# TensorE in the order of the source inside a latent-attention stage, with maxima, turns and keys at other places

## The chip, the cores and the metric

The kernel runs on one core of a Trainium2 chip. A core has five engines, each with its own queue of instructions: TensorE (PE) for matrix products and transposes, VectorE (DVE), ScalarE (ACT), GpSimd (POOL) and SyncE (SP), which here starts most of the transfers (DMA). Engines wait for each other by semaphores. PE writes to PSUM, a small memory of eight banks, here one tile `PB` of eight banks of 512 floats for each of 128 partitions; In this kernel DVE and ACT read PSUM, POOL does not. All else lies in SBUF, here mostly in two large tiles, `arena_r` and `arena_f`. The metric is the time of one execution in microseconds (us), lower is better.

## The reference

A backbone of two layers over 1024 latent tokens and 256 context tokens, width 1024. Layer 0 is windowed attention, layer 1 latent attention; each adds its gated result to the stream. The change touches layer 1 alone:

```python
q = (rms_norm(cq, q_norm) @ w_uq).reshape(b, n, B_HEADS, B_NOPE + B_ROPE)
kv = (rms_norm(ckv, kv_norm) @ w_ukv).reshape(b, n, B_HEADS, B_NOPE + B_V)
...
s = (jnp.einsum("bqhd,bkhd->bhqk", qn, kn)
     + jnp.einsum("bqhd,bkd->bhqk", qr, kr)).astype(F32) * scale
p = jax.nn.softmax(s, axis=-1).astype(v.dtype)
return jnp.einsum("bhqk,bkhd->bqhd", p, v)
```

There are 16 heads; a query and a key have 64 entries of their own and 32 rotated ones, a value has 64. Each of the 1024 latent queries sees all 1280 keys, context first. The result is multiplied by a gate, projected by `w_out`, added to the stream and normalised.

## The kernel before, in words

The first thousand microseconds compute layer 0 and the projections of layer 1. The stage of the change starts near 1000 us and ends near 1540; the output projection of the last tiles follows.

In this stage the work is cut into 32 units (class `UnitB`). Unit `i` is one head and one half of the queries (512): two heads make a pair, so four units in a row belong to one pair of heads, in the order head 0 first half, head 0 second half, head 1 first half, head 1 second half. A unit does, in terms of the code's names:

- `prep`: loads the queries, already split into a high and a low part (two DMAs).
- `top(b)`, four times, for 128 queries each: three matmuls (L1294) into banks 0 to 2 give rough scores against all 1280 keys, and DVE takes their maximum in one reduction over 1280 columns (L1298). All tops share the same three banks, so a top has to wait until the reduction of the one before has read them.
- `shift`: a transpose (L1302) turns the maxima, and four short ACT instructions (L1305) write them as extra rows of the queries, so that the scores come out already lowered by the maximum.
- `score(c)` for the ten chunks of 128 keys: three matmuls (`mm3`, L126, L127, L128: high by high, low by high, high by low) into one of the banks 3, 4, 5 in turn, then the exponential on ACT (L1313), then an addition on POOL (L1317, L1320) that sums the denominators.
- `PV`: ten matmuls (L1328) of the exponentials with the values into bank 6. Each takes half of PE's columns, even chunks the lower and odd chunks the upper half.
- `fin`: a copy on ACT (L1342) and an addition on DVE (L1343) join the two halves.
- `fin2`: four transposes (L1353) of the summed denominators, which need POOL's last addition, a sum on DVE (L1354) and, for the second head of a pair, a reciprocal and two copies on ACT (L1357, L1362).
- `fin3`, for the second head of a pair alone: four transposes (L1371), a product on DVE (L1372), a product with the gate on POOL (L1374) and a store.

The loop over the units lays these out over the ten scores `c` of a unit: tops and shift of the next unit, `fin2` and `fin3` of the one before, and the next pair's keys. `make_K` makes those in the third unit of a pair, in three pieces of 512, 512 and 256 keys (`KEYB`): for each piece two `mm3` write one bank with both heads, 64 partitions each, and for each head a cast on ACT (L121) and a subtraction on DVE (L122) split it. `make_V` makes the values of four heads in every eighth unit, in five pieces. Banks are handed out in turn by the objects `pst4` (3, 4, 5), `psv` (6) and `psx` (7, for the transposes).

Order: the framework records the instructions and its scheduler sets the order on every engine by its own costs and priorities, unless a part of the kernel is put under `tc.manual_schedule`, in which the engines named keep the order of the source. An earlier stage is under it, this one is not. Waits on semaphores are then placed by the framework wherever two instructions use the same place in a tile.

Of the kernel before, what the change touches and what calls it, by code (L numbers as in the profile page):

```python
# [33 lines left out]
class Ring:  # L34
# [6 lines left out]
    def next(self):  # L41
        b = self.bufs[self.i % len(self.bufs)]
        self.i += 1
        return b
# [15 lines left out]
def kernel(ctx: ExitStack, tc: tile.TileContext, t, out, dbg=None):  # L60
    nc = tc.nc
# [57 lines left out]
    def split(hi, lo, src, lo_eng=None):  # L119

        nc.scalar.copy(hi, src)  # L121
        (lo_eng or nc.vector).tensor_sub(lo, src, hi.bitcast(F32))  # L122

    def mm3(o, a, b, first, last):
        (ah, al), (bh, bl) = a, b
        nc.tensor.matmul(o, ah, bh, start=first, stop=False)  # L126
        nc.tensor.matmul(o, al, bh, start=False, stop=False)  # L127
        nc.tensor.matmul(o, ah, bl, start=False, stop=last)  # L128
# [345 lines left out]
    psv = Banks(5)  # L474
# [390 lines left out]
    in_order = tc.manual_schedule()  # L865
# [45 lines left out]
    for ui, u in enumerate(units):  # L911
# [7 lines left out]
        nu = units[ui + 1] if ui + 1 < len(units) else None  # L919
# [299 lines left out]
    pst4 = Banks(3, 4, 5)  # L1219
    psv = Banks(6)  # L1220
# [18 lines left out]
    def make_V(quad):  # L1239
        for tp in range(NP):  # L1240
            ps = pst4()
            for j in range(2):
                ti = 2 * tp + j
                for k in range(2):
                    mm3(
                        ps[:, j * 256 : j * 256 + 256],
                        [ckvT[:, s, k, ti * 128 : ti * 128 + 128] for s in range(2)],
                        [ukV[:, s, k, quad * 256 : quad * 256 + 256] for s in range(2)],
                        k == 0, k == 1,
                    )  # L1250
            nc.scalar.copy(Vq[:, 2 * tp : 2 * tp + 2], shp(ps, 2, 4, 64))
            yield

    def make_K(pair):
        for n0, n in KEYB:
            ps = pst4()
            for k in range(2):
                mm3(
                    ps[:, 0:n],
                    [ukK[:, s, k, pair * 128 : pair * 128 + 128] for s in range(2)],  # L1260
                    [ckvT[:, s, k, n0 : n0 + n] for s in range(2)],
                    k == 0, k == 1,
                )
            for e in range(2):
                kt = kTb[(2 * pair + e) % 3]
                split(kt[0:64, 0, n0 : n0 + n], kt[0:64, 1, n0 : n0 + n], ps[64 * e : 64 * e + 64, 0:n])
            yield
# [119 lines left out]
    def wo_pieces():  # L1387
        ring = Ring(F, [45, 47, 49], 512)
        pieces = [(k, slice(c * 512, c * 512 + 512)) for k in range(8) for c in range(2)]
        staged = []  # L1390
        for i in range(len(pieces) + 2):
            if i < len(pieces):
                k, cs = pieces[i]
                st = ring.next()
                load(out=st, in_=t["b_w_out"][k * 128 : k * 128 + 128, cs])
                staged.append((k, cs, st))
            if i >= 2:
                k, cs, st = staged.pop(0)
                split(WoB[k][:, 0, cs], WoB[k][:, 1, cs], st)
                yield  # L1400
# [102 lines left out]
    for _ in make_K(0):  # L1503
        pass
# [30 lines left out]
    out_fill = out_tiles()  # L1535
    wo_fill = wo_pieces()
    kfill = vfill = iter(())
    for ui, u in enumerate(units):
        pu = units[ui - 1] if ui else None
        nu = units[ui + 1] if ui + 1 < NU else None  # L1540
        nnu = units[ui + 2] if ui + 2 < NU else None
        if ui % 4 == 2 and u.pair < 7:
            kfill = make_K(u.pair + 1)
        if ui and ui % 8 == 0:
            vfill = make_V(u.pair // 2)
        for c in range(NT):
            if nu and ui and c in (1, 4, 6):
                nu.top({1: 1, 4: 2, 6: 3}[c])
            if nu and c == 8:
                nu.shift()  # L1550
            if nnu and c == 3:
                nnu.prep()
            u.score(c)
            if nnu and c == 9:
                nnu.top(0)
            if c == 9:
                u.PV()
                u.fin()
            if pu and c == 3:
                pu.fin2()  # L1560
            if pu and c == 5:
                pu.fin3()
            if ui % 4 == 2 and c in (1, 3, 5):
                next(kfill, None)
            if ui and ui % 8 == 0 and c in (1, 2, 4, 6, 7):
                next(vfill, None)
            if ui % 2 and 3 <= ui < 25 and c == 0 or 25 <= ui < 29 and c in (0, 5):
                next(wo_fill, None)
            if ui == NU - 1 and c in (0, 3, 5, 6, 7, 8, 9):
                next(out_fill, None)  # L1570
    for _ in wo_fill:
        pass
    u = units[-1]
# [81 lines left out]
```

## Time and profile before

| | |
|---|---|
| median of three runs | 1631.81 us (1630.6 to 1632.72) |
| profiled execution, its time | 1630.86 us |
| its span | 1628.6 us |
| PE busy over the span | 1577.6 us (97%) |
| DVE, ACT, POOL busy | 947.7, 803.8, 815.5 us |
| 1100 to 1200 us: PE, DVE, ACT, POOL busy | 99.78, 52.14, 55.56, 68.42 us |

The profile is one execution. Busy time of PE is the time in which a matmul was under way; successive matmuls overlap, so their lengths add up to more than the time from start to start. In the records each matmul of L1328 appears twice, so ten of them are x20. The granted clock is the share of its full clock that PE was given; it is 1.00 for nearly all of the run and lower in a few short stretches.

### The profile page before, as it was taken

The page shows a single profiled execution, that of the slowest core. Times are in us where ns is not written, and L with a number is a line of the kernel's source. Part 1 is how long each engine was busy: PE and PEld are TensorE (multiplying, and loading weights), DVE is VectorE, ACT ScalarE, POOL GpSimd, SP SyncE. Part 2 cuts the span into 40 slices and gives each one's busy share as a digit, 9 for nine tenths or more (in the row PEclk, how much of TensorE's full clock was granted, in tenths as well). Part 3 has the DMA queues.
Part 4 walks back from the last instruction along what each step waited for, and adds up shares of the span by engine and source line. Part 5 has one row for each costly group of instructions (what it writes and reads, how often), then busy time and mean ns, then how long its engine had stood idle before and what let it go on. Part 6 is the DMA issues. An engine that isn't in the chain of part 4 may idle for free.

```text
span 1628.6 us, 23522 instructions
## 1 busy us (share of the span) xinstructions
PE 1577.6 (97%) x8156; PEld 1213.2 (74%) x8156; DVE 947.7 (58%) x1719; ACT 803.8 (49%) x1715; POOL 815.5 (50%) x871
## 2 busy tenths in 40 slices
PE   6899999989999999999999999999999999999998
PEld 2788788777888888878887887566666666666687
DVE  2766778637777777768353016655545455455354
ACT  2511221249777777777233335555555555555421
POOL 2653355235453333335154423686777768668410
PEclk8999999989999999999999999999999999999999
DMA  8435644564343333243138613111110110122151
GB/s 302 159 124 176 205 145 152 175 187 120 95 142 97 92 92 91 78 147 120 45 107 281 188 55 110 55 56 33 40 56 20 55 33 33 56 72 70 47 162 65
DMA packets 122430, 176.72 MB, mean 109 GB/s; under 512 B 11452, under 2 KB 71484, under 8 KB 122312
## 3 DMA queue, kind: packets, MB, share of 16 engines
q1 hardware_dynamic: 115032, 164.31, 31.7%
q10 hardware_dynamic: 7280, 10.92, 2.1%
q8 instruction: 64, 1.05, 0.3%
q14 instruction: 54, 0.44, 0.1%
HBM read 129.04 MB, written 46.15 MB: 108 GB/s over the span
## 4 chain that ended last, share of the span: by engine, by line
PE 82%; ACT 4%; DVE 4%; issue 3%; DMA 3%; POOL 3%; SPq 0%; ACTq 0%; POOLq 0%; DVEq 0%
PE PB L126 18%; PE PB L128 17%; PE PB L127 17%; PE PB L1328 9%; PE PB L570 5%; PE PB L1294 4%; PE PB L560 4%; PE PB L533 2%; PE PB L534 2%; DMA arena_f<-a_w_in 1%; PE PB L1353 1%; DVE arena_f L344 1%; ACT arena_f L581 1%; ACT arena_f L1313 1%; DMA arena_f<-x 1%
## 5 line engine op out<-in xcount | busy, mean ns | idle before, releaser
L126 PE MATMUL PB<-arena_r 128*128 128x512 f32 (+3 forms) x1632 | 608.6, 373 | 3.3 <-ACT arena_r L205 2.1
L127 PE MATMUL PB<-arena_r 128*128 128x512 f32 (+3 forms) x1632 | 596.8, 366 | 2.9 <-POOL arena_r L727 2.2
L128 PE MATMUL PB<-arena_r 128*128 128x512 f32 (+3 forms) x1632 | 595.0, 366 | 0.2 <-DVE arena_r L122 0.2
L126 PEld LDWEIGHTS PB<-arena_r 128*128 128x128 f32 (+1 forms) x1632 | 310.7, 190 | 91.6 <-issue 32.9
L1320 POOL TENSOR_TENSOR arena_f<-arena_f 128x512 f32<-128x512 f32 x252 | 327.1, 1298 | 75.1 <-ACT arena_f L1313 60.0
L128 PEld LDWEIGHTS PB<-arena_r 128*128 128x128 f32 (+1 forms) x1632 | 310.0, 190 | 49.0 <-DVE arena_r L122 0.4
L127 PEld LDWEIGHTS PB<-arena_r 128*128 128x128 f32 (+1 forms) x1632 | 310.9, 191 | 45.1 <-POOL arena_r L727 2.7
L1298 DVE TENSOR_REDUCE arena_f<-PB 128x1 f32<-128x1280 f32 x128 | 190.4, 1487 | 104.2 <-PE PB L1294 101.7
L1313 ACT ACTIVATE arena_f<-PB 128x512 f32<-128x512 f32 x320 | 189.0, 597 | 125.2 <-PE PB L128 112.8
L122 DVE TENSOR_TENSOR arena_r<-PB,arena_r 128x512 fp32r<-128x512 f32 (+4 forms) x245 | 158.7, 655 | 124.2 <-ACT arena_r L121 122.4
L122 POOL TENSOR_TENSOR arena_r<-arena_f,arena_r 128x512 fp32r<-128x512 f32 x80 | 111.3, 1405 | 173.1 <-ACT arena_r L121 169.5
L121 ACT CAST arena_r<-PB 128x512 fp32r<-128x512 f32 (+4 forms) x245 | 135.4, 557 | 68.1 <-PE PB L560 39.3
L540 DVE CUSTOM_DVE_ANT_0 arena_f<-PB,arena_f,small 128x256 f32<-128x256 f32 (+1 forms) x288 | 145.4, 523 | 32.1 <-PE PB L534 25.3
L1328 PE MATMUL PB<-arena_f 128*64 128x512 f32 x640 | 157.1, 600 | 0.0
L541 ACT ACTIVATE arena_f<-arena_f,small 128x640 f32<-128x640 f32 (+2 forms) x160 | 118.9, 744 | 27.8 <-DVE small L540 26.9
L570 PE MATMUL PB<-arena_r 128*128 128x512 f32 x336 | 120.8, 436 | 4.5 <-ACT arena_f L581 4.1
L344 DVE SCALAR_TENSOR_TENSOR arena_f<-arena_f,small 128x512 f32<-128x512 f32 x98 | 116.3, 1231 | 2.6 <-DMA arena_f<-ada_w 2.2
L121 ACT CAST arena_r<-arena_f 128x512 fp32r<-128x512 f32 (+1 forms) x120 | 69.7, 608 | 76.8 <-DMA arena_f<-a_w_in 26.4
L560 PE MATMUL PB<-ident,arena_f 128*128 128x128 f32 x672 | 104.9, 273 | 0.5 <-ACT arena_f L541 0.3
L1328 PEld LDWEIGHTS PB<-arena_f 128*64 128x64 f32 x640 | 43.6, 136 | 80.9 <-issue 79.5
L1294 PE MATMUL PB<-arena_r 96*128 96x512 f32 (+1 forms) x384 | 99.8, 368 | 0.3 <-DVE arena_f L1298 0.2
L560 PEld LDWEIGHTS PB<-ident,arena_f 128*128 128x128 f32 x672 | 82.6, 140 | 15.0 <-ACT arena_f L541 1.5
(163 smaller groups left out, 1723.0 us busy)
## 6 DMA issues: line engine op xcount, KB each, us to landing
arena_r<-q_d SPq DMA_DIRECT2D x148, 128.0 KB, 2.9
arena_f<-ada_w SPq DMA_DIRECT2D x64, 256.0 KB, 3.3
arena_f<-a_w_in SPq DMA_DIRECT2D x40, 256.0 KB, 3.1
arena_f<-ada_w SPq DMA_DIRECT2D x16, 512.0 KB, 7.3
arena_f<-x SPq DMA_DIRECT2D x16, 512.0 KB, 3.5
q_d<-arena_f SPq DMA_DIRECT2D x16, 512.0 KB, 3.5
qn_d<-arena_f SPq DMA_DIRECT2D x16, 512.0 KB, 5.7
arena_r<-qn_d SPq DMA_DIRECT2D x32, 256.0 KB, 3.5
```

The source lines that it names most:

```text
L121: nc.scalar.copy(hi, src)
L122: (lo_eng or nc.vector).tensor_sub(lo, src, hi.bitcast(F32))
L126: nc.tensor.matmul(o, ah, bh, start=first, stop=False)
L127: nc.tensor.matmul(o, al, bh, start=False, stop=False)
L128: nc.tensor.matmul(o, ah, bl, start=False, stop=last)
L560: nc.tensor.transpose(pt[:, h, :], self.Ps[h][:, ci * 128 : ci * 128 + 128], ident)
L570: nc.tensor.matmul(self.pv, V[:, self.chunks[ci], self.g, :], PT[:, s], start=ci == 0 and s == 0, stop=ci == self.m - 1 and s == 1,)
L1294: nc.tensor.matmul(psm[:, n0 : n0 + n], self.qT[0:96, 0, b * 128 : b * 128 + 128], kt[0:96, 0, n0 : n0 + n], start=True, stop=True,)
L1298: nc.vector.reduce_max(self.mx[:, 96 + b : 97 + b], psm[:, 0:TOK], AX.X, negate=True)
L1313: nc.scalar.activation(E, S, AF.Exp)
L1320: eng.tensor_add(self.acc, self.acc, E)
L1328: nc.tensor.matmul(self.pv[p : p + 64], Vq[:, c, self.h % 4, :], self.E.pop(c), start=c < 2, stop=c >= NT - 2)
```

## The change

It has three parts.

First, the loop over the units is put under `tc.manual_schedule` for PE alone: PE now does what the source says, in that order; the scheduler still orders DVE, ACT, POOL and SP, now around a fixed PE. Second, calls move within the loop, and so on PE: the second, third and fourth top (`top(1)`, `top(2)`, `top(3)`) come before scores 1, 3, 5 instead of 1, 4, 6, `shift` before score 9 instead of 8, `fin2` before score 2 instead of after 3, `fin3` before score 6 instead of after 5, the three pieces of keys after scores 2, 4, 7 instead of 1, 3, 5. Third, from the second pair on the keys are written to bank 6 (`psv`), which the product with the values uses, instead of one of the three banks of the scores.

```diff
     def make_K(pair):
         for n0, n in KEYB:
-            ps = pst4()
+            ps = pst4() if pair == 0 else psv()
...
+    in_order = tc.manual_schedule(engines={nc.tensor.engine})
+    in_order.__enter__()
     for ui, u in enumerate(units):
...
         for c in range(NT):
-            if nu and ui and c in (1, 4, 6):
-                nu.top({1: 1, 4: 2, 6: 3}[c])
-            if nu and c == 8:
+            if pu and c == 2:
+                pu.fin2()
+            if pu and c == 6:
+                pu.fin3()
+            if nu and ui and c in (1, 3, 5):
+                nu.top({1: 1, 3: 2, 5: 3}[c])
+            if nu and c == 9:
                 nu.shift()
...
             if c == 9:
                 u.PV()
                 u.fin()
-            if pu and c == 3:
-                pu.fin2()
-            if pu and c == 5:
-                pu.fin3()
-            if ui % 4 == 2 and c in (1, 3, 5):
+            if ui % 4 == 2 and c in (2, 4, 7):
                 next(kfill, None)
...
+    in_order.__exit__(None, None, None)
```

What this does to the order, at three places. On PE, the end of a unit that makes keys and the next unit's first scores; L1328 is the product with the values, 128x512 in L126 to L128 a score. Before:

```order
L1328 MATMUL PB<-arena_f 64x512 x6
L126 MATMUL PB<-arena_r 128x512
L127 MATMUL PB<-arena_r 128x512
L128 MATMUL PB<-arena_r 128x512
L1328 MATMUL PB<-arena_f 64x512
L126 MATMUL PB<-arena_r 128x512
L127 MATMUL PB<-arena_r 128x512
L128 MATMUL PB<-arena_r 128x512
L1328 MATMUL PB<-arena_f 64x512 x2
```

After:

```order
L1302 MATMUL PB<-ident,arena_f 100x128
L126 MATMUL PB<-arena_r 128x512
L127 MATMUL PB<-arena_r 128x512
L128 MATMUL PB<-arena_r 128x512
L1294 MATMUL PB<-arena_r 128x512 x2
L1294 MATMUL PB<-arena_r 128x256
L1328 MATMUL PB<-arena_f 64x512 x10
```

Two scores of the next unit and a single matmul stood inside the product; now the shift's transpose, the last score and the first top of the unit after next stand ahead of it, and its ten matmuls follow each other.

On PE, the second and third top of an ordinary unit (L1294). Before:

```order
L1294 MATMUL PB<-arena_r 128x512 x2
L1294 MATMUL PB<-arena_r 128x256
L126 MATMUL PB<-arena_r 128x512
L127 MATMUL PB<-arena_r 128x512
L128 MATMUL PB<-arena_r 128x512
L126 MATMUL PB<-arena_r 128x512
L127 MATMUL PB<-arena_r 128x512
L128 MATMUL PB<-arena_r 128x512
L126 MATMUL PB<-arena_r 128x512
L127 MATMUL PB<-arena_r 128x512
L1294 MATMUL PB<-arena_r 128x512 x2
L1294 MATMUL PB<-arena_r 128x256
```

After:

```order
L1294 MATMUL PB<-arena_r 128x512 x2
L1294 MATMUL PB<-arena_r 128x256
L126 MATMUL PB<-arena_r 128x512
L127 MATMUL PB<-arena_r 128x512
L128 MATMUL PB<-arena_r 128x512
L126 MATMUL PB<-arena_r 128x512
L127 MATMUL PB<-arena_r 128x512
L128 MATMUL PB<-arena_r 128x512
L1294 MATMUL PB<-arena_r 128x512 x2
L1294 MATMUL PB<-arena_r 128x256
```

Eight matmuls of scores stood between the two tops, now six.

On DVE, a unit that makes keys, from the second top's maximum (L1298) on; L122 with 64x512 or 64x256 is the subtraction that ends the split of one head's piece of keys, L1354 the sum of `fin2`. Before:

```order
L122 TENSOR_TENSOR arena_r<-PB,arena_r 64x512
L1354 TENSOR_REDUCE small<-PB 128x4
L122 TENSOR_TENSOR arena_r<-PB,arena_r 64x512
L1298 TENSOR_REDUCE arena_f<-PB 128x1
L122 TENSOR_TENSOR arena_r<-PB,arena_r 64x512
L1298 TENSOR_REDUCE arena_f<-PB 128x1
L122 TENSOR_TENSOR arena_r<-PB,arena_r 64x512
L122 TENSOR_TENSOR arena_r<-PB,arena_r 64x256
L1298 TENSOR_REDUCE arena_f<-PB 128x1
L122 TENSOR_TENSOR arena_r<-PB,arena_r 64x256
```

After:

```order
L1354 TENSOR_REDUCE small<-PB 128x4
L1298 TENSOR_REDUCE arena_f<-PB 128x1
L122 TENSOR_TENSOR arena_r<-PB,arena_r 64x512 x2
L1298 TENSOR_REDUCE arena_f<-PB 128x1
L122 TENSOR_TENSOR arena_r<-PB,arena_r 64x512 x2
L122 TENSOR_TENSOR arena_r<-PB,arena_r 64x256 x2
L1298 TENSOR_REDUCE arena_f<-PB 128x1
```

The first piece's two subtractions stood ahead of the second top's maximum and now stand behind it; those of the second piece stand behind the third top's maximum, and the last piece's ahead of the first maximum of the unit after next. On ACT the second cast of each piece stands behind the exponential of a score that PE reaches just before the next piece (score 4, score 7) or just before the shift (score 8).

## The prediction

> **What bounds the kernel now.** I read the busy shares first, then the table of windows for four neighbouring units, then the timelines of TensorE (PE), VectorE (DVE) and ScalarE (ACT) inside a unit. A row of windows gives the stretch, its length, the busy time and count of PE, weight loads, DVE, ACT and POOL, the granted clock, DMA share and GB/s; a row of a timeline gives start, length, engine, line, what it does, and the idle time before it with what ended it.
>
> ```profile
> span 1628.6 us, 23522 instructions
> PE 1577.6 (97%) x8156; PEld 1213.2 (74%) x8156; DVE 947.7 (58%) x1719; ACT 803.8 (49%) x1715; POOL 815.5 (50%) x871
> 1199.04:1214.29 15.25, 15.12 (x72) 9.69 (x72) 8.05 (x8) 8.38 (x19) 12.74 (x11) 1.00 0.19 61
> 1214.29:1228.74 14.45, 14.45 (x68) 9.31 (x67) 7.24 (x6) 7.68 (x17) 11.91 (x11) 1.00 0.19 65
> 1228.74:1263.86 35.12, 35.01 (x157) 21.75 (x156) 18.89 (x20) 18.85 (x40) 23.89 (x19) 1.00 0.08 23
> 1199.04:1263.86 64.82, 64.57 (x295) 40.75 (x294) 34.19 (x34) 34.92 (x72) 48.54 (x39) 1.00 0.13 41
> ```
>
> PE is busy 64.57 of 64.82 us in a group of four units at full clock, and DVE about half. So time can be won only where PE's own work gets shorter, and any wait of PE is lost in full. The profiled execution took 1630.86 us, 2.3 beyond its span and 0.95 below the median of the runs, 1631.81.
>
> One ordinary unit on PE, from one product with the values (L1328, ten instructions, two records each) to the next, with DVE's reductions (L1298: a maximum; L1354: the sum in fin2) behind it:
>
> ```profile
> 1214.29 4.51 PE L1328 MATMUL PB<-arena_f 128*64 128x512 f32 x20
> 1218.73 0.50 PE L126 MATMUL PB<-arena_r 100*128 100x512 f32 x1
> ...
> 1219.53 0.73 PE L1294 MATMUL PB<-arena_r 96*128 96x512 f32 x3
> 1220.10 0.40 PE L126 MATMUL PB<-arena_r 100*128 100x512 f32 x1
> ...
> 1222.17 0.60 PE L1353 MATMUL PB<-ident,arena_f 128*128 128x128 f32 x4
> 1222.53 0.84 PE L1294 MATMUL PB<-arena_r 96*128 96x512 f32 x3
> 1223.20 0.39 PE L126 MATMUL PB<-arena_r 100*128 100x512 f32 x1
> 1223.43 0.39 PE L127 MATMUL PB<-arena_r 100*128 100x512 f32 x1
> ...
> 1225.05 0.75 PE L1294 MATMUL PB<-arena_r 96*128 96x512 f32 x3
> ```
> ```profile
> 1219.55 0.68 DVE L1343 TENSOR_TENSOR arena_f<-PB,arena_f 64x512 f32<-64x512 f32 x1 [3.66 <-ACT arena_f L1342]
> 1222.81 0.69 DVE L1354 TENSOR_REDUCE small<-PB 128x4 f32<-128x512 f32 x1 [1.01 <-PE PB L1353]
> 1223.42 1.48 DVE L1298 TENSOR_REDUCE arena_f<-PB 128x1 f32<-128x1280 f32 x1
> 1225.84 1.49 DVE L1298 TENSOR_REDUCE arena_f<-PB 128x1 f32<-128x1280 f32 x1 [0.94 <-PE PB L1294]
> ```
>
> Starts of following rows give PE's prices: 4.44 for ten value products, 0.80 for the first score of a unit, 0.57 for a top, 0.69 for a score (three matmuls of 0.23), 0.36 for fin2's four transposes. The round trip of a top: started at 1225.05, its reduction starts 0.79 later and takes 1.49; the earlier reduction ended at 1224.90 and the next top started 0.15 after that. Start to start, two tops need 0.79 + 1.49 + 0.15 = 2.43 us, which leaves 1.86 between the end of one and the start of the next. Before, 2.67 scores stand there (1223.20 to 1225.05, 1.85 us).
>
> **The value product in one run (a gain).** In the units that make keys the run was cut:
>
> ```profile
> 1243.95 1.07 PE L1328 MATMUL PB<-arena_f 128*64 128x512 f32 x2
> 1244.95 0.32 PE L1302 MATMUL PB<-ident,arena_f 128*100 128x128 f32 x1
> ...
> 1247.21 2.80 PE L1328 MATMUL PB<-arena_f 128*64 128x512 f32 x12
> 1249.94 0.50 PE L126 MATMUL PB<-arena_r 100*128 100x512 f32 x1
> ...
> 1250.83 1.07 PE L1328 MATMUL PB<-arena_f 128*64 128x512 f32 x2
> 1251.83 0.50 PE L126 MATMUL PB<-arena_r 100*128 100x512 f32 x1
> ...
> 1252.73 1.08 PE L1328 MATMUL PB<-arena_f 128*64 128x512 f32 x4
> 1253.74 0.85 PE L1294 MATMUL PB<-arena_r 96*128 96x512 f32 x3
> ```
>
> The pieces cost 1.00 + 2.73 + 1.00 + 1.01 = 5.74 against 4.44: two neighbours share their time, one alone pays for both. That is 1.30 a group. I take the whole possible gain from the group: four units of 14.45, keys of 12 x 0.23 + 6 x 0.12 = 3.5, and fin3's four transposes twice at fin2's 0.36 make 62.0; before takes 64.82. So 2.8 is the most that order can win, fin3's stall included (15.25 - 14.45 - 0.36 = 0.44 each, twice). Units 0 and 1 were cut as 1 + 9, which saves about 1.0 each.
>
> **Maxima at scores 1, 3, 5 (a loss).** Counted from the unit's first score: first top at 0.80, S1, fin2 at 2.06, S2, so the second top could start at 3.11. The first reduction runs 1.59 to 3.08, so the top starts at 3.23. Its reduction runs 4.02 to 5.51 (fin2's sum, 3.08 to 3.77, is out of its way), so the third top starts at 5.66, where two scores would let it start at 3.23 + 0.57 + 1.38 = 5.18. Waits: 0.12 + 0.48 = 0.60, less 0.1 for a switch cost between L1353 and L1294 (0.67 where 0.57 is usual) that goes away: 0.5 in each of the three units of a group that make no keys, 1.5 a group. A unit with values has their matmuls between the tops, so there this is an upper bound.
>
> **Fin2 at score 2, fin3 at 6 (nothing).** Fin2's transposes need POOL's last add, and PE now waits for it in order.
>
> ```profile
> 1215.90 1.27 POOL L1374 TENSOR_TENSOR arena_f<-arena_f,arena_r 128x512 f32<-128x512 f32 x1
> 1217.14 2.62 POOL L1320 TENSOR_TENSOR arena_f<-arena_f 128x512 f32<-128x512 f32 x2
> ```
>
> The last add ends at 1219.76, 1.03 after the score at 1218.73; fin2 comes at 2.06. The cover is 1.0 us. POOL's gating multiply of fin3 and its store to DRAM come two adds earlier: the same work on POOL and SP, and the later adds still end before 2.06. If that cover went, each microsecond late would be PE's. Fin3 stands 3.5 us behind fin2, past its sum, reciprocal and copies. The shift one score later has top 0 and the value product, 5 us, ahead of the next unit's scores.
>
> **Keys in the bank of the product (the large loss).** Three scores shared three banks with the keys; now each piece of keys has one bank, and the next piece (then the value product) must wait until both heads of the last are split.
>
> ```profile
> 1236.85 0.58 ACT L121 CAST arena_r<-PB 64x512 fp32r<-64x512 f32 x1 [0.73 <-PE PB L128]
> 1238.23 0.58 ACT L121 CAST arena_r<-PB 64x512 fp32r<-64x512 f32 x1
> ```
> ```profile
> 1237.46 0.68 DVE L122 TENSOR_TENSOR arena_r<-PB,arena_r 64x512 fp32r<-64x512 f32 x1 [1.21 <-ACT arena_r L121]
> 1239.40 0.69 DVE L122 TENSOR_TENSOR arena_r<-PB,arena_r 64x512 fp32r<-64x512 f32 x1
> ```
>
> Cast, subtraction, cast, subtraction go one after the other: the second cast starts 0.08 after the first subtraction ends (1238.15), so 0.58 + 0.03 + 0.69 + 0.08 + 0.58 + 0.03 + 0.69 = 2.7 us. In the new order DVE takes the second top's reduction first, and ACT takes the second cast of piece 1 behind the exponential of score 7. By the clock of the unit: piece 0 at 3.11 to 4.50, the second top at 4.50, its reduction 5.29 to 6.78, subtraction to 7.47, cast to 8.13, subtraction to 8.85, piece 1 at 9.00. PE would be there at 5.08 + 1.38 = 6.46: a wait of 2.5. Piece 1 ends at 10.39, the third top at 10.97, S5 to S7 at 13.04; the exponential of S7 ends near 13.9, cast 14.5, subtraction 15.22, piece 2 at 15.37: 2.3. Piece 2 ends at 16.09, S8 16.78, S9 and the top 18.2; its second cast, behind the exponential of S8, ends at 18.03 and the subtraction of 0.42 at 18.48, the product starts at 18.63: 0.4. Sum 5.2 a group. Between ends: nothing, if DVE and ACT took the splits at once and two scores hid them, and about 6, if each exponential in ACT's way came late; I take 5.2, since the rows show the chain's length.
>
> **Clock after a wait.** The granted clock drops for 3.41 us after a stretch of 3.41 with much idle time:
>
> ```profile
> 69.67:73.09 3.42, 1.66 (x14) 1.66 (x15) 3.29 (x8) 2.72 (x5) 2.39 (x2) 1.00 0.04 13
> 73.09:76.50 3.41, 3.41 (x31) 3.41 (x30) 3.32 (x8) 1.25 (x2) 0.78 (x2) 1.00 0.00 0
> 342.74:346.15 3.41, 1.52 (x9) 0.97 (x8) 0.00 (x0) 0.23 (x1) 0.00 (x0) 1.00 1.10 250
> 346.15:349.56 3.41, 0.00 (x0) 0.00 (x0) 0.76 (x2) 1.50 (x3) 0.20 (x1) 0.50 1.13 218
> 738.68:742.09 3.41, 1.28 (x10) 1.08 (x10) 3.41 (x7) 2.67 (x6) 1.99 (x4) 1.00 0.32 89
> 742.10:745.51 3.41, 3.18 (x14) 2.83 (x14) 3.17 (x4) 3.06 (x8) 3.24 (x3) 0.50 0.12 38
> ```
> ```profile
> 741.58 0.37 PE L126 MATMUL PB<-arena_r 128*128 128x288 f32 x1 [2.12 <-ACT arena_r L205]
> ```
>
> Idle 1.76 (69.67) left it at 1.00; idle 1.89 and 2.13 led to 0.50. The keys' waits leave PE idle for some 2.35 and 2.15 (the last matmul runs 0.16 past its slot). At a random place against the grid of 3.41, at least 1.8 of that falls into one stretch with a chance of (3.41 - 1.8 + 0.55 or 0.35) / 3.41, about 0.6: eight of 14 waits. A slow stretch puts off the next wait and with it its place on the grid, so the waits are not independent; I take five of 14, between none and eight. Each costs at most half of 3.41, about 1.6: 8 us.
>
> [...]
>
> **Sum.** A group goes from 64.8 to 62.0 + 5.2 + 1.5 = 68.7, or 3.9 slower. Seven groups make keys: +27. Units 0 and 1 save 2; the last group, with one unit for maxima less and uncut products, loses about 1. Together +26, and +8 for the clock: 1630.86 + 34 = 1665, beside the median some 1666; I give 1665.
>
> **Rivals.**
> - The waits as above, the clock always full: 1630.9 + 26, about 1658. For it: 1.76 us of idle time did no harm. Chance 0.22.
> - Nearly every long wait halves the clock, some for two stretches: 14 x 1.6 = 22, so 1680. For it: 342.74 was followed by more than one. Against: PE is busy after each wait. Chance 0.10.
> - The keys wait about once a unit (2.5), because DVE finishes the subtractions ahead of the reductions: 1630.9 + 7 x 1.2 - 1 + clock 3, about 1642. Against: DVE runs in its order. Chance 0.08.
> - Faster: the splits fit between the pieces, so that the keys' waits are gone and the single run is kept: 62.0 + 1.5 - 64.8 = -1.3 a group, -9, and -1 at the ends: 1621. It decides where the keys' waits are below 1.3 a group, against the 5.2 worked out. Against: 2.7 us of chain plus 1.5 of reduction have 1.95 us of cover. Chance 0.05.
>
> **Numbers.** Forecast 1665 with 0.55. The range 1648 to 1677 leaves out the slow end, the faster case and most of the once-a-unit case. Less than 0.2% (3.3 us) counts as no change, about what a measurement here can tell: faster 0.05, same 0.02, slower 0.93.
>
> **What would show it.** Right: TensorE idle before the second and third pieces of keys, 2 to 2.5 us each, released by DVE L122; 0.1 and 0.5 before the second and third top, released by L1298; L1328 x20 everywhere; half-clock stretches between 1000 and 1540 us. Wrong: no such idle time, or fin2 waiting for POOL, or a span of four units near 62.

## The result, and the profile after

The changed kernel takes 1672.08 us (median of 4 runs, 1666.57 to 1675.58) against 1632.26 (4 runs, 1630.6 to 1633.2): 1.0242 times as long, 95% interval 1.0211 to 1.0273. The profiled execution took 1670.25 us. Its busy shares, page of the changed kernel:

```profile
span 1668.5 us, 23538 instructions
PE 1580.7 (95%) x8156; PEld 1223.1 (73%) x8156; DVE 943.0 (57%) x1719; ACT 807.3 (48%) x1715; POOL 816.4 (49%) x871
```

The span is 39.9 us longer, PE's busy time only 3.1, so PE is idle for 36.8 of them. (Busy time alone hides two things that nearly cancel, both below: less work in cut products, and matmuls that take longer at half clock, as an L127 of a score, 0.63 us from 1192.01 at 0.50 against 0.39 from 1116.05 at 1.00.) Four units, from the product of unit 3 to that of unit 7 (ordinary with fin3, ordinary, keys, ordinary with fin3, then the sum), and a unit with keys elsewhere; columns as in the prediction's windows:

```profile
1070.14:1085.54 15.40, 15.21 (x72) 9.64 (x71) 8.06 (x8) 8.35 (x19) 12.79 (x11) 1.00 0.22 62
1085.54:1100.46 14.92, 14.73 (x69) 9.26 (x68) 7.25 (x6) 7.69 (x17) 12.19 (x11) 1.00 0.23 63
1100.46:1123.41 22.95, 18.52 (x87) 12.21 (x86) 10.68 (x13) 10.64 (x22) 14.18 (x12) 1.00 0.05 17
1123.41:1138.77 15.36, 15.17 (x71) 9.63 (x72) 8.03 (x8) 8.47 (x19) 9.36 (x8) 1.00 0.09 27
1175.76:1201.56 25.80, 21.60 (x87) 14.62 (x86) 10.65 (x12) 10.92 (x24) 14.43 (x12) 0.87 0.06 16
1070.14:1138.77 68.63, 63.62 (x295) 40.74 (x295) 34.02 (x34) 35.16 (x72) 48.52 (x39) 1.00 0.14 39
```

The group takes 68.63 us against 64.82 before; in the unit with keys PE is busy 18.52 of 22.95 us. The same work at a lower clock takes 25.80. Who waited for whom on PE between 1030 and 1545 us (total, times, longest):

```profile
PE PB L126 <- DVE arena_r L122: 29.4, 14, 2.1
PE PB L1294 <- DVE arena_f L1298: 4.4, 18, 1.1
PE PB L1328 <- DVE arena_r L122: 0.9, 4, 0.2
```

The fourteen waits are those of the second and third pieces of keys in seven units, 2.12 and 2.08 us. One of the first kind, on DVE, ACT and PE:

```profile
1110.26 1.49 DVE L1298 TENSOR_REDUCE arena_f<-PB 128x1 f32<-128x1280 f32 x1 [1.70 <-PE PB L1294]
1111.67 0.67 DVE L122 TENSOR_TENSOR arena_r<-PB,arena_r 64x512 fp32r<-64x512 f32 x1
1112.99 0.69 DVE L122 TENSOR_TENSOR arena_r<-PB,arena_r 64x512 fp32r<-64x512 f32 x1 [0.65 <-ACT arena_r L121]
```
```profile
1112.38 0.58 ACT L121 CAST arena_r<-PB 64x512 fp32r<-64x512 f32 x1
```
```profile
1109.48 0.74 PE L1294 MATMUL PB<-arena_r 96*128 96x512 f32 x3
...
1113.74 0.50 PE L126 MATMUL PB<-arena_r 128*128 128x512 f32 x1 [2.12 <-DVE arena_r L122]
```

Reduction of the second top, subtraction, second cast, second subtraction: each starts where the one before ends, and the second piece of keys starts at 1113.74, right behind them. It was due at 1111.45, one matmul's 0.23 after the last one, which started at 1111.22. The third piece's wait ends in another way: its second cast stands on ACT behind the exponentials of three scores,

```profile
1116.77 1.98 ACT L1313 ACTIVATE arena_f<-PB 128x512 f32<-128x512 f32 x3 [0.75 <-PE PB L128]
1118.77 0.58 ACT L121 CAST arena_r<-PB 64x512 fp32r<-64x512 f32 x1
```

and starts when they end, 0.68 us after the first subtraction had ended (1118.09). There the order on ACT sets the length, as the prediction had it.

The clock, in four stretches of 3.41 us in a row:

```profile
1187.12:1190.53 3.41, 1.49 (x6) 1.24 (x7) 1.22 (x2) 1.07 (x2) 2.47 (x2) 1.00 0.00 0
1190.54:1193.95 3.41, 3.41 (x10) 2.73 (x9) 2.08 (x2) 1.18 (x2) 0.05 (x1) 0.50 0.00 0
1193.95:1197.36 3.41, 1.33 (x7) 0.80 (x7) 0.69 (x1) 1.78 (x3) 3.25 (x3) 1.00 0.00 0
1197.37:1200.78 3.41, 3.41 (x13) 2.80 (x12) 0.42 (x1) 1.34 (x4) 0.80 (x2) 0.50 0.00 0
```

Each of the two waits of this unit (1.92 and 2.08 us idle within its stretch) is followed by a stretch at half clock, and the unit is 25.80 - 22.95 = 2.85 longer, 1.43 for each. There are eight such stretches in the stage, seven behind waits for keys and one at its start. Only seven of the fourteen waits have one. The others are cut by the end of a stretch in such a way that no stretch is idle for more than 1.76 us; so it is with the wait that ends at 1113.74, and the stretch after it keeps the full clock:

```profile
1112.03:1115.44 3.41, 1.70 (x7) 1.43 (x8) 1.00 (x2) 0.87 (x3) 2.26 (x2) 1.00 0.00 0
1115.44:1118.85 3.41, 2.61 (x12) 1.81 (x10) 2.08 (x2) 2.46 (x5) 1.28 (x1) 1.00 0.00 0
```

### The profile page after: what moved, and what is told of

It reads as the page before. It is cut to its first block, busy times and chain, and to the rows that moved or that the text cites. A ratio compares the mean times of both kernels' runs of the same rounds, so it can differ in the third digit from the quotient of the medians.

```text
span 1668.5 us, 23538 instructions
## 1 busy us (share of the span) xinstructions
PE 1580.7 (95%) x8156; PEld 1223.1 (73%) x8156; DVE 943.0 (57%) x1719; ACT 807.3 (48%) x1715; POOL 816.4 (49%) x871
## 4 chain that ended last, share of the span: by engine, by line
PE 78%; DVE 7%; ACT 5%; POOL 4%; issue 4%; DMA 2%; POOLq 0%; ACTq 0%; SPq 0%; DVEq 0%
PE PB L126 17%; PE PB L127 16%; PE PB L128 16%; PE PB L1328 8%; PE PB L570 5%; PE PB L1294 5%; PE PB L560 4%; DVE arena_f L1298 2%; PE PB L533 2%; PE PB L534 2%; DVE arena_r L122 1%; ACT arena_r L121 1%; PE PB L674 1%; PE PB L1353 1%; ACT arena_f L1313 1%
## 5 line engine op out<-in xcount | busy, mean ns | idle before, releaser
L126 PE MATMUL PB<-arena_r 128*128 128x512 f32 (+3 forms) x1632 | 617.7, 379 | 34.4 <-DVE arena_r L122 29.4
L127 PE MATMUL PB<-arena_r 128*128 128x512 f32 (+3 forms) x1632 | 600.4, 368 | 3.1 <-POOL arena_r L727 2.2
L128 PE MATMUL PB<-arena_r 128*128 128x512 f32 (+3 forms) x1632 | 599.3, 367 | 0.1
L126 PEld LDWEIGHTS PB<-arena_r 128*128 128x128 f32 (+1 forms) x1632 | 313.8, 192 | 123.0 <-DVE arena_r L122 35.7
L128 PEld LDWEIGHTS PB<-arena_r 128*128 128x128 f32 (+1 forms) x1632 | 313.1, 192 | 50.1 <-DVE arena_r L122 0.3
L127 PEld LDWEIGHTS PB<-arena_r 128*128 128x128 f32 (+1 forms) x1632 | 313.7, 192 | 42.9 <-POOL arena_r L727 2.7
L1298 DVE TENSOR_REDUCE arena_f<-PB 128x1 f32<-128x1280 f32 x128 | 190.8, 1491 | 133.9 <-PE PB L1294 129.6
L122 DVE TENSOR_TENSOR arena_r<-PB,arena_r 128x512 fp32r<-128x512 f32 (+4 forms) x245 | 158.8, 655 | 136.7 <-ACT arena_r L121 135.6
L122 POOL TENSOR_TENSOR arena_r<-arena_f,arena_r 128x512 fp32r<-128x512 f32 x80 | 111.4, 1407 | 175.5 <-ACT arena_r L121 164.3
L1328 PE MATMUL PB<-arena_f 128*64 128x512 f32 x640 | 144.4, 597 | 0.9 <-DVE arena_r L122 0.9
L1294 PE MATMUL PB<-arena_r 96*128 96x512 f32 (+1 forms) x384 | 100.3, 370 | 4.9 <-DVE arena_f L1298 4.9
L1328 PEld LDWEIGHTS PB<-arena_f 128*64 128x64 f32 x640 | 43.1, 136 | 82.5 <-issue 80.1
```

The source lines that it names most:

```text
L1294: nc.tensor.matmul(psm[:, n0 : n0 + n], self.qT[0:96, 0, b * 128 : b * 128 + 128], kt[0:96, 0, n0 : n0 + n], start=True, stop=True,)
L1298: nc.vector.reduce_max(self.mx[:, 96 + b : 97 + b], psm[:, 0:TOK], AX.X, negate=True)
L1328: nc.tensor.matmul(self.pv[p : p + 64], Vq[:, c, self.h % 4, :], self.E.pop(c), start=c < 2, stop=c >= NT - 2)
```

## The experiments

The theory: PE in the order of the source loses every wait of an instruction at its head; the long ones are those for the splits of the keys, and the idle time they make halves the clock now and then. The rivals: the order is neutral and the places or the bank cost by themselves; the clock costs nothing. Two reference points serve for all: before, 1631 to 1632 us, and the changed kernel, 1672.

**The fixed order alone.** The kernel before, with nothing but this:

```diff
+    in_order = tc.manual_schedule(engines={nc.tensor.engine})
+    in_order.__enter__()
     for ui, u in enumerate(units):
...
+    in_order.__exit__(None, None, None)
```

> The kernel before with one part of the change alone: TensorE keeps the order of the source, with all calls at their old places and the keys in the scores' three banks. Theory (a TensorE that may not step past a waiting instruction loses every wait, and the scheduler had been steering around them): slower than before by 30 to 55 us, with TensorE idle before the tops, before fin2 (released by POOL L1320) and in the units that make keys. Rival (the order itself is the gain, the new places and the bank are the loss): the 2.8 us a group of the uncut product come through, 1610 to 1615 us, and no new idle time on TensorE.

Measured: 1685.78 us, 1.0327 times before (1.0311 to 1.0342), 53 us slower and 14 slower than the whole change. PE's waits between 1030 and 1545 us:

```profile
PE PB L126 <- DVE arena_r L122: 25.4, 14, 2.1
PE PB L1371 <- ACT arena_f L1362: 12.8, 11, 1.2
PE PB L1302 <- DVE arena_f L1298: 3.6, 17, 0.2
PE PB L1294 <- DVE arena_f L1298: 1.2, 6, 0.2
```

The fixed order by itself loses more than the whole change; the rival, that the order is the gain, falls. The keys wait nearly as in the changed kernel (25.4 us against 29.4), and fin3, at its old place two scores behind fin2, waits 1.2 us for ACT's copies (L1362), which the change's new place takes away. Fin2 did not wait for POOL in this stretch, against the expectation.

**The bank undone.**

```diff
-            ps = pst4() if pair == 0 else psv()
+            ps = pst4()
```

> The changed kernel with the keys back in the scores' banks 3 to 5; order and places stay. Theory of the prediction (the single bank is what makes the pieces wait): the 5.2 us in each of seven groups go, with the clock's 8 x 1.4 us, so about 1672 - 47 = 1625 us. Rival (the length of the chain reduction, subtraction, cast, subtraction is what counts, and in a fixed order some score then waits for the bank that a piece of keys holds): the same within some 12 us of the changed kernel, unit of 22.5 to 23.5 us, idle time before scores in place of pieces of keys.

Measured: 1671.94 us, 1.0243 (1.0222 to 1.0265): the same as the changed kernel. So the prediction's own theory fell here. PE in a unit with keys:

```profile
1115.70 0.50 PE L126 MATMUL PB<-arena_r 128*128 128x512 f32 x1 [2.12 <-DVE arena_r L122]
...
1122.97 0.50 PE L126 MATMUL PB<-arena_r 100*128 100x512 f32 x1 [2.08 <-DVE arena_r L122]
```

The first wait is again the second piece of keys (128 rows): between two pieces stand two scores, and in a ring of three banks the next piece gets the bank of the last one. The second wait is now that of a score (100 rows), S7, which gets the bank of the second piece. The bank has changed who waits and not how long.

**The tops undone**, at scores 1, 4, 6:

```diff
-            if nu and ui and c in (1, 3, 5):
-                nu.top({1: 1, 3: 2, 5: 3}[c])
+            if nu and ui and c in (1, 4, 6):
+                nu.top({1: 1, 4: 2, 6: 3}[c])
```

> The changed kernel with the tops back at scores 1, 4, 6. Theory 1 (the tops cost what the prediction says, 1.5 us a group): 8 x 1.5 = 12 us less, about 1660. Theory 2 (the second top's reduction, which DVE does ahead of the first piece's subtractions, is also what delays the keys): besides the waits between tops, the unit with keys gets some 1.5 to 2 us shorter, its waits fall below what halves the clock, and the time is about 1672 - 18 - 11 = 1643.

Measured: 1647.96 us, 1.0109 (1.0086 to 1.0132), 24 less than the changed kernel, twice what the prediction's 1.5 a group comes to. DVE and PE in a unit with keys:

```profile
1102.76 0.68 DVE L122 TENSOR_TENSOR arena_r<-PB,arena_r 64x512 fp32r<-64x512 f32 x1 [1.73 <-ACT arena_r L121]
1103.42 1.49 DVE L1298 TENSOR_REDUCE arena_f<-PB 128x1 f32<-128x1280 f32 x1
1104.94 0.69 DVE L122 TENSOR_TENSOR arena_r<-PB,arena_r 64x512 fp32r<-64x512 f32 x1
```
```profile
1105.69 0.50 PE L126 MATMUL PB<-arena_r 128*128 128x512 f32 x1 [1.60 <-DVE arena_r L122]
...
1112.48 0.39 PE L126 MATMUL PB<-arena_r 128*128 128x256 f32 x1 [0.92 <-DVE arena_r L122]
```

The reduction of the second top now stands between the two subtractions instead of ahead of both, and the waits are 1.60 and 0.92 instead of 2.12 and 2.08; the mean granted clock of the profiled execution is 0.988 against 0.981. Theory 2 holds: where a top stands also decides when the keys' bank is free.

**The long waits filled with work.** Four matmuls whose result nothing reads, ahead of the second and of the third piece:

```diff
             if ui % 4 == 2 and c in (2, 4, 7):
+                if c > 2 and u.pair < 7:
+                    for _ in range(4):
+                        nc.tensor.matmul(PB[:, 7, :], ukK[:, 0, 0, 0:128], ckvT[:, 0, 0, 0:512], start=True, stop=True)
                 next(kfill, None)
```

> The changed kernel with four more matmuls (128x512, result not read by anything) before the second and before the third piece of keys, in bank 7, which is free there: 0.9 us of work put into each of the two long waits of a unit with keys. Theory (the waits' length comes from DVE and ACT, and the half clock from the idle time): the waits of 2.1 us show as 1.2 idle, no half-clock stretches between 1030 and 1540 us, and 8 x 1.4 = 11 us less, about 1661. Rival (the granted clock costs nothing on the path, or is set by something else): half-clock stretches as before and 1672 or more.

Measured: 1657.63 us, 1.0160 (1.0144 to 1.0175): 56 more matmuls, and 14 us less than without them.

```profile
1110.01 0.50 PE L126 MATMUL PB<-arena_r 128*128 128x512 f32 x1 [1.19 <-DVE arena_r L122]
1116.43 0.39 PE L126 MATMUL PB<-arena_r 128*128 128x256 f32 x1 [1.15 <-DVE arena_r L122]
...
1030.00:1540.00 510.00, 487.43 (x2332) 322.70 (x2329) 247.78 (x247) 260.38 (x516) 346.94 (x272) 1.00 0.15 44
```

Every unit with keys takes 22.96 to 22.99 us now, as the undisturbed ones did, the idle time of a wait is 1.2 us where it was 2.1, and the mean granted clock of the stretch is 1.00 where it was 0.98. So here the waits' length came from DVE and ACT, and the half clock from PE's idle time. This also gives the waits without the clock: 1657.6, 25 us above before.

**The keys' second piece in another bank.** In the code the second piece goes to bank 7 and the first and third to bank 6; the expectation names the banks otherwise, so its 1643 was worked out for another edit.

```diff
-            ps = pst4() if pair == 0 else psv()
+            ps = pst4() if pair == 0 else (psx if n0 == 512 else psv)()
```

> The changed kernel with the keys' two large pieces in banks 7 and the small one in bank 6... in the code: pieces of 512 in bank 7 (psx), the piece of 256 in bank 6. Theory (a piece waits because the bank it needs is unread; the second large piece still follows the first in bank 7, but the third and the product with the values find bank 6 free): the second wait and the product's wait go, about 2.5 of 4.9 us a unit, and no two waits stand in one unit, so some 17 us and the clock's 11 less: about 1643. If the scheduler also gives DVE another order around the pieces, the first wait can go too: unit near 18.4 us, about 1626. Rival (DVE's and ACT's own time for the splits is what PE pays for, whatever the banks): the unit with keys stays at 22 to 23 us and the time at 1655 to 1672.

Measured: 1627.03 us, 0.9966 (0.9953 to 0.9979): 45 less than the changed kernel and below before. Between 1030 and 1545 us PE's waits are:

```profile
PE PB L1294 <- DVE arena_f L1298: 4.6, 19, 1.1
PE PB L1328 <- DVE arena_r L122: 1.6, 7, 0.2
```

No piece of keys waits any more, the units with keys take 18.22 us, and the mean granted clock from 1030 to 1500 us is 1.00. The tops' waits are those of the changed kernel (4.4 there). The expectation's 1626, given for another order on DVE, agrees in the number alone: DVE still does the second top's reduction (from 1104.32) ahead of the first piece's subtractions, and it is the second bank that takes the wait away.

**The waits between the tops gone too.** As above, and

```diff
-            if pu and c == 2:
+            if pu and c == (4 if ui == 1 else 2):
                 pu.fin2()
...
-            if nu and ui and c in (1, 3, 5):
-                nu.top({1: 1, 3: 2, 5: 3}[c])
-            if nu and c == 9:
-                nu.shift()
+            if nu and ui and c in (1, 4, 7):
+                nu.top({1: 1, 4: 2, 7: 3}[c])
...
             u.score(c)
+            if nu and c == 9:
+                nu.shift()
```

> All waits taken away that the runs so far showed: keys as in e5, tops at scores 1, 4, 7 (at least two scores and fin2 or three scores between two tops), shift after score 9, fin2 in the second unit two scores later. Theory (the order of the source is no loss in itself once every waiting instruction has its 2.4 us, and the uncut product's gain then comes through): units of 14.4 and 14.8, with keys 18.4, no half clock in the stage: a group of 62.0 against 64.8, seven or eight times 2.8 less some 4 for fin3's switches and the start: 1612 to 1620. Rival (TensorE in fixed order costs something that no wait shows): 1630 or more.

Measured: 1619.26 us, 0.9920 (0.9908 to 0.9933), faster than both kernels. Four units, as the sum above:

```profile
1064.98:1127.50 62.52, 62.30 (x295) 41.38 (x294) 34.29 (x34) 35.00 (x71) 48.52 (x39) 1.00 0.15 43
```

62.5 against the prediction's 62.0 for work without waits, and 64.8 before: the fixed order is no loss where every waiting instruction finds its data there. Against the expectation, waits stay at the ends of the stage: 1.6 us for POOL before fin2 in the second unit (1021.68), 1.6 for a maximum before a shift (1029.30), and 1.0 for POOL in the last group (1484.99).

**One bank, tops spaced.** The last kernel with the changed kernel's bank for all pieces, and fin2 at score 2 in all units:

```diff
-            ps = pst4() if pair == 0 else (psx if n0 == 512 else psv)()
+            ps = pst4() if pair == 0 else psv()
```

> The changed kernel with its single bank for the keys, but tops at scores 1, 4, 7 and the shift after score 9. Theory 1 (the bank costs by itself, by the chain of two casts and two subtractions): the unit with keys stays some 2 us above its work of 17.9, about 20.5, ordinary units at 14.4 and 14.8, so a group near 64.3 and the time about the kernel's before, 1628 to 1638. Theory 2 (the place of the tops is the whole loss): 1612 to 1620, as e6.

Measured: 1635.77 us, 1.0024 (1.0014 to 1.0034).

```profile
1108.75 0.50 PE L126 MATMUL PB<-arena_r 128*128 128x512 f32 x1 [1.61 <-DVE arena_r L122]
1116.47 4.51 PE L1328 MATMUL PB<-arena_f 128*64 128x512 f32 x20 [0.21 <-DVE arena_r L122]
```

One long wait, of 1.6, is left in the units with keys (20.5 us), and 16.5 us of time beside the spaced kernel: theory 1 in its size. Its chain is not only casts and subtractions, though. DVE in front of that wait:

```profile
1105.80 0.68 DVE L122 TENSOR_TENSOR arena_r<-PB,arena_r 64x512 fp32r<-64x512 f32 x1 [1.75 <-ACT arena_r L121]
1106.48 1.49 DVE L1298 TENSOR_REDUCE arena_f<-PB 128x1 f32<-128x1280 f32 x1
1108.00 0.69 DVE L122 TENSOR_TENSOR arena_r<-PB,arena_r 64x512 fp32r<-64x512 f32 x1
```

The second top's reduction still stands between the two subtractions. In a fixed order a single bank does cost, as long as two scores and a top cannot cover that chain; what the bank would cost without the reduction in it was not run.

**The bank alone, order free.** The kernel before with only the changed line of `make_K`:

> The kernel before with one part of the change alone: from the second pair on the keys are written to bank 6; TensorE is ordered by the scheduler, the calls at their old places. Theory (a bank's wait costs only where TensorE may not step past it, and the scheduler puts scores of the next unit into the gap): within 10 us of before, 1628 to 1642, product with the values still cut in the units with keys. Rival (the bank costs the chain of two casts and two subtractions in any order, some 4 us in each of seven units): 1655 or more.

Measured: 1637.05 us, 1.0036 (1.0024 to 1.0049), 6 us slower. PE has no wait for L122 among its longest; it waits for POOL before fin2, 0.7 us in each unit with keys, which the new order of the scheduler brings. The product of these units is not cut, against the expectation; that of the unit behind each is, as 1 + 9:

```profile
PE PB L1353 <- POOL arena_f L1320: 5.1, 7, 0.8
```

**Places and bank, order free.** The changed kernel without the two lines of the fixed order:

> The changed kernel without the fixed order: places and bank as changed, TensorE ordered by the scheduler again. Theory (the fixed order turns the waits into idle time, so the scheduler gets most of them back): 1645 to 1660, below the changed kernel's 1672. Rival (the places and the bank by themselves make the loss, the order is neutral): the same as the changed kernel within 5 us, 1667 to 1677.

Measured: 1659.13 us, 1.0166 (1.0150 to 1.0183).

```profile
PE PB L1353 <- POOL arena_f L1320: 14.3, 8, 1.9
PE PB L1294 <- DVE arena_f L1298: 10.0, 7, 1.5
```

The scheduler sets PE in another order, in which other instructions wait: fin2 for POOL and a top for its bank. It gets back 13 us of 40, no more. Places and bank thus cost 28 us without the fixed order too, by other waits, and the parts do not add up: 53 for the order alone, 28 for places and bank, 40 for all. Why the scheduler chose that order stays open.

## Why the prediction was right or wrong

The time lay in the range, the direction and most of the sum held. By its steps:

- *Keys in the bank of the product, 5.2 a group*: the size was right. The unit with keys took 22.95 us, against 14.45 + 3.5 + 5.2 = 23.15; the waits left PE idle 2.12 and 2.08 us where 2.35 and 2.15 were given, and the product waited 0.2 instead of 0.4. The name of the cause was wrong in part. With the keys back in the scores' ring the time was the same, since two scores between two pieces bring the ring of three round to the same bank. What costs is a fixed order with a chain on DVE and ACT that is longer than PE's work up to the next use of the bank, whether that is the one bank or one of the ring of three.
- *Maxima at scores 1, 3, 5, 1.5 a group*: the sum held (units of 14.92 against 14.95 worked out), its parts less so. In the unit from 1085.54 the second top does not wait (0.12 given), and the third starts 0.36 late (0.48 given). The 0.15 from a reduction's end to the next top had been read where PE was not waiting; here the reduction from 1093.99 ends at 1095.48 and the top starts at 1095.54. The keys' chain was worked out with the second top's reduction in it, but its cost was put down to the bank alone; undoing the tops gave 24 us and not 12.
- *The gain of the order, up to 2.8 a group, 1.3 of it the value product in one run*: the product is in one run everywhere (x20), and the spaced kernel shows 2.3 of the gain, 62.5 against 64.8. In the changed kernel the waits take more than that: without the clock, five groups took 371.73 - 6 x 1.43 = 363.1 us against 344.64, 3.7 slower a group where 3.9 was forecast:

```profile
1127.36:1472.00 344.64, 343.82 (x1652) 225.78 (x1651) 174.69 (x174) 184.59 (x371) 243.47 (x191) 1.00 0.15 46
```
```profile
1138.77:1510.50 371.73, 347.91 (x1651) 232.94 (x1650) 174.63 (x174) 186.49 (x371) 243.79 (x191) 0.97 0.14 42
```

- *Clock after a wait, five of 14 at 1.6, 8 us*: mis-sized. The profiled execution had seven such stretches behind the 14 waits of 2.08 to 2.12 us and one behind a wait of 1.83 at the start of the stage; at 1.43 each that is 11.4, and the filled kernel's median was 14.5 less. The eight of 14 worked out at first was nearer than the five chosen from it; each cost a little less than the 1.6 given. The first rival, no cost of clock at 1658, fell: only with the waits filled did the kernel take 1657.6.
- *Fin2 at score 2, nothing*, and *units 0 and 1 save 2*: wrong for the start. In unit 1 PE waited for POOL's last addition:

```profile
1020.03 1.12 PE L1353 MATMUL PB<-ident,arena_f 128*128 128x128 f32 x4 [1.83 <-POOL arena_f L1320]
```

  The cover of 1.0 us had been read from a unit in the middle of the stage, and unit 1 stands at its start. The stretch after it, from 1019.87, ran at 0.50 too. Before, with fin2 two scores later, PE had already waited there, which the prediction did not look at:

```profile
1018.65 0.66 PE L1353 MATMUL PB<-ident,arena_f 128*128 128x128 f32 x4 [0.50 <-POOL arena_f L1320]
```

  So one of the signs of being wrong did show, in this unit alone; in all others the cover held.
- *The last group, about 1*: from the product of unit 27 to that of unit 31 it took 68.5 against 67.3 us, 1.2 slower.

So 1665 was 7 too low. Of the 39.9 us between the two spans, 1.6 lie ahead of the first top of the stage (970.8 against 969.2), where the change does nothing, 6.0 between there and the product of unit 3, 30.9 in the six groups that follow, 1.2 in the last group and 0.2 behind it. Against the forecast of 34 the clock is 3.4 more (11.4 for 8), the start without its clock about 1 more, the six groups without theirs about 1 less. The median of the runs lies another 1.8 above the profiled execution.

## What to carry to other kernels

Before an engine's order is fixed, work out for each instruction at its head what it waits for, in time from the last use of its buffer: here a top could start 2.3 us after the start of the one before (1093.20 to 1095.54), and a piece of keys 4.3 us after the last matmul of the one before was through (1109.48 to 1113.74), where the splits share DVE with a reduction. A ring of buffers gives no protection when the number of uses between two slow ones is one less than its length. Here two waits of TensorE in one unit, 2.12 and 2.08 us, cost 2.85 us beyond their length, and 56 matmuls that nothing reads took 14 us off the time; best was a second buffer and more distance, which turned 2.4% slower into 0.8% faster. The order, the places and the buffers have to be chosen together: the order alone, the bank alone, and places and bank together were each slower than before.

## What the runs showed of the hardware

The granted clock went with PE's idle time in the stretch of 3.41 us before. In the changed kernel's stage the seven stretches at full clock that were idle for 1.92 to 2.12 us were all followed by one at 0.50. In the traces of the kernel before and of the changed one, from 30 to 1560 us, so were all thirteen stretches at full clock that were idle for 1.89 us or more, and none that was idle for 1.53 or less; between the two it went either way. Two stretches of the changed kernel, each with what followed:

```profile
1016.46:1019.87 3.41, 1.74 (x8) 1.09 (x7) 2.17 (x2) 3.03 (x6) 3.25 (x3) 1.00 0.32 106
1019.87:1023.29 3.42, 3.26 (x10) 2.77 (x11) 1.29 (x2) 0.60 (x1) 1.36 (x3) 0.50 0.00 0
1405.58:1408.99 3.41, 1.65 (x7) 1.39 (x8) 1.05 (x2) 0.91 (x2) 2.31 (x2) 1.00 0.00 0
1408.99:1412.40 3.41, 2.66 (x13) 1.85 (x11) 2.08 (x2) 2.41 (x5) 1.28 (x1) 1.00 0.00 0
```

And one of the kernel with the tops undone:

```profile
1102.69:1106.10 3.41, 1.81 (x9) 1.19 (x8) 2.84 (x3) 1.82 (x4) 2.73 (x3) 1.00 0.00 0
1106.10:1109.51 3.41, 3.41 (x10) 2.64 (x9) 0.58 (x1) 0.58 (x1) 0.16 (x1) 0.50 0.00 0
```

1.67 us of idle time (1016.46) and 1.60 (1102.69) were followed by 0.50, 1.76 (1405.58) by 1.00. What beside the idle time decides there stays open. A stretch at half clock cost 1.43 us in the changed kernel (2.85 for two), a little under half of 3.41. The changed kernel spread over 9 us in four runs and the one with the waits filled over 4, but the fixed order alone, whose profiled execution has the same mean clock as the changed kernel's, 0.981, over 5; whether the clock makes the spread stays open.
